# Softmax divided on a^T behind the attention, position tables fetched during the fold, full-height Fourier tails

## Chip, cores and metric

The kernel runs on one core of a Trainium2 chip. The metric is device time in microseconds for one execution of the whole program, which is one encoder layer on two request batches. All of it is computed in fp32 precision: each operand of a large matmul is split into a rounded high part and a remainder, and three matmuls replace one (high times high, high times low, low times high).

## The reference, cut to what matters

```python
def encoder_layer(x, ...):                    # x_prompt: 256 + 16 meta tokens, x_sample: 1024 + 16, d_model 1024
    h = rms_norm(x, norm_mix_g)
    z = h @ w_in                              # q 512 | k 128 | v 128 | f 512 | gate logits 1024 + 1024
    ...
    g_attn = jax.nn.sigmoid(z[..., o3:o4]); g_four = jax.nn.sigmoid(z[..., o4:])
    q = axial_rope(head_rms_norm(q, q_norm_g), row, col); k = ...     # 8 query heads, 2 kv heads, head_dim 64
    a = bidirectional_gqa(q, k, v) @ w_attn_o
    fo = fourier_mix(f) @ w_four_o
    x = x + (g_attn * a + g_four * fo) @ w_out
    h2 = rms_norm(x, norm_ffn_g); u = h2 @ w_ffn_in                   # d_ff 2816
    return x + (jax.nn.silu(u[..., :D_FF]) * u[..., D_FF:]) @ w_ffn_out

def attention_block(qb, k, v):
    s = jnp.einsum('bqhgd,bshd->bhgqs', qb, k) * scale
    p = jax.nn.softmax(s, axis=-1)
    return jnp.einsum('bhgqs,bshd->bqhgd', p, v)

def fourier_mix(f):                           # 4 groups of 128 channels
    return jnp.real(jnp.fft.fftn(f.reshape(b, l, 4, 128), axes=(1, 3), norm='ortho')).reshape(b, l, 512)
```

## The kernel before

The work runs in stages. Tokens stand in three chunks: 0 and 1 are the 1024 sample tokens, 2 the 256 prompt tokens; tiles 0 to 7 are the sample's 128-row tiles, 8 and 9 the prompt's. Most tiles in on-chip memory are slots of one pool, and a new user of a slot waits for the last user of the old one. The order of instructions on an engine is the order in which the program's generators write them, except inside manual blocks, where it is written out; `weave` and `Filler` mix a main generator with a side generator by cost shares. SyncE (SP) issues most DMAs, one queue in order; GpSimd (POOL) issues the position tables.

- Up to 65 us the tokens are normalized and transposed (hT). `folds` adds and subtracts mirrored positions (tiles ep, od, then eo as high and low parts). `fourier_in` multiplies these with the channel matrix wc into six banks u, and then casts the banks into `ue` and `uo` (the even and odd parts, high on ScalarE, low on VectorE). The fifth bank has 41 rows.
- `fourier` multiplies the position tables with ue and uo: `tabp` for the prompt (outputs fpe, fpo, rows 128 and 41), `tabc` and `tabs` for the sample (fse and so on, rows 4 x 128 and 9). Their DMAs are issued behind fourier_in, `tabs` at the second of the kinds. `gate_gen` makes the gate logits g, one unit of weights (wg, cast to wgh, remainder wgl) at a time: chunk 0 is woven into the Fourier, q and kv passes (shares 0.6, 0.35, 0.7), chunks 1 and 2 fill the attention by `FILL`, in ns per yield.
- Attention handles the prompt tiles first, then the sample. For a tile, a kv group g and four heads it makes the scores S (one buffer), their negated maximum (L954), the exponential p with its row sum (L961), and, one head later, `scale`: a reciprocal (L965) and p times it (L966). `Second` and `product` then transpose p (pt, pT) and multiply with v (pv, ao), and store a^T to a_d.
- `load_af` reads a_d back and splits it (afh, afl) for the merge; chunks 0 and 2 are started at the end of the attention, chunk 1 inside the merge. `merge` runs over eight column blocks i: `fourier(i + 1)` (fo), then m for chunks 0, 2, 1; `need` prepares the weights wm two blocks ahead, behind the first m. `w_out` follows; its first weight unit is split by GpSimd (woh, wol).
- ffn_in and ffn_out fill the time from 905 us to the end.

Of the kernel before, what the change touches and what calls it, by code (L numbers as in the profile page):

```python
# [9 lines left out]
F32 = mybir.dt.float32  # L10
F32R = mybir.dt.float32r
# [125 lines left out]
def f32(ap):  # L137
    return ap.bitcast(F32)
# [44 lines left out]
class Kernel:  # L183
    def __init__(self, tc, nc, a, o, pools):
        self.tc, self.nc, self.a, self.o = tc, nc, a, o
        self.const, self.small, self.dram, big = pools
        self.later = None
        self.sl = Slots(big, N_SLOTS, N_TRIPLES)
        c = self.const
        self.ident = c.tile([P, P], F32, name="ident")  # L190
        nc.scalar.dma_start(self.ident[:], a["ident"])
        self.gcol = c.tile([P, KD], F32, name="gcol")
        self.mhalf = c.tile([P, NQH], F32, name="mhalf")
        nc.vector.memset(self.mhalf[:], -0.5)
        self.gates = [
            [self.dram.tile([P, n], F32, name=f"gate{u}_{i}") for i, n in enumerate(CH_N)]
            for u in range(16)
        ]
        self.x_d = [self.dram.tile([P, D], F32, name=f"x_d{t}") for t in range(10)]
        self.act_d = [[self.dram.tile([P, 640], F32, name=f"act_d{j}_{k}") for k in range(NH)] for j in range(7)]  # L200
        self.q_d = [self.dram.tile([P, D], F32, name=f"q_d{t}") for t in range(10)]
        self.a_d = [self.dram.tile([512, n], F32, name=f"a_d{i}") for i, n in enumerate(CH_N)]


        self.f_d = self.dram.tile([516, NL], F32, name="f_d")
# [291 lines left out]
            yield  # L497
        sl.put(*hs, ep, od)

    def fourier_in(self, ps):  # L500

        nc, sl = self.nc, self.sl
        cols = [(j * P, P) for j in range(4)] + [(512, 41), (553, P)]
# [1 line left out]
        for k in range(KD):  # L505
# [16 lines left out]
                sl.put(*x)  # L522
            if k + 2 < KD:
                next(self.fold)
            if k % 2:
                sl.put(*self.wc[k // 2])
        next(self.fold, None)
        ue = [sl.get("ue", F32R) for _ in range(3)]
        uo = [sl.get("uo", F32R) for _ in range(3)]
        for x in uo:  # L530
            nc.gpsimd.memset(f32(x.v(4, 256))[:, :, 252:256], 0.0)
        for j, (_, m) in enumerate(cols):
            ev = banks[j][:m, :260].rearrange("p (g c) -> p g c", g=4)
            b = j % 2 * 520
            u = ue[j // 2]
            for base, w, src in ((0, 64, ev[:, :, :64]), (256, 1, ev[:, :, 64:65])):
                hv = u.v(4, w, b + base)[:m]
                lv = u.v(4, w, b + 260 + base)[:m]
                nc.scalar.copy(hv, src)
                nc.vector.tensor_tensor(lv, src, f32(hv), op=ALU.subtract)  # L540
            b = j % 2 * 512
            u = uo[j // 2]
            src = banks[j][:m, 260:512]
            nc.scalar.copy(u[:m, b : b + 252], src)
            nc.vector.tensor_tensor(u[:m, b + 256 : b + 508], src, f32(u[:m, b : b + 252]), op=ALU.subtract)
        self.U = ue, uo
        yield 6000

    FILL = {"s": 455, "p": 350, "end": 480, "drain": 900}

    def gate_gen(self, chunks, lo_engine):

# [56 lines left out]
    def fourier(self, ps):  # L611
        nc, a, sl = self.nc, self.a, self.sl
        tp = [sl.get(f"tabp{j}", F32R) for j in range(2)]
        for j, m in enumerate((P, 41)):
            nc.gpsimd.dma_start(tp[j][:m, : 4 * NLP], a["pos_p"][j, :m])
        yield from self.fourier_in(ps)
        us = self.U

        def u_e(uu, j, m, p, part):
# [24 lines left out]
            nc.sync.dma_start(self.f_d[row : row + m, lo : lo + n], st[:m, :n])  # L644


        ms = [P, 41]
        for kind, p in kinds:
            rows = 4 if kind == "4" else P
            pf = ps.tile([P, 512], F32, tag="mm", name=f"fp{kind}{p}")  # L650
# [12 lines left out]
        sl.put(*tp)  # L663


        ms = [P, P, P, P, 9]
        tabs = {}

        def tab(name):
            tabs[name] = [sl.get("tab" + name, F32R) for _ in range(5)]  # L670
            for j, m in enumerate(ms):
                nc.gpsimd.dma_start(tabs[name][j][:m, :1040], a["pos_" + name][j, :m])

        tab("c")
        for i, (kind, p) in enumerate(kinds):
            if i == 1:
                tab("s")
# [173 lines left out]
    def attention(self, ps, tiles, tag_s, tag_v):  # L851
# [64 lines left out]
            )  # L916
            sl.put(aos)

        queue, n, scale, S = deque(), 0, None, None

        def turns(k):

# [9 lines left out]
        for i, (t, g) in enumerate(units):  # L932
# [5 lines left out]
                seq, L, cuts = "p", LP, (0, LP)  # L938
            per = SLOT // L
            ps4, slots = [], []  # L940
            for h in range(4):
                hq = q[t][:, (4 * g + h) * P : (4 * g + h + 1) * P]

# [9 lines left out]
                nb, total, rc = sm[:, 0:1], sm[:, 1:2], sm[:, 2:3]  # L953
                nc.vector.tensor_reduce(nb, S[:, base : base + L], axis=AX.X, op=ALU.max, negate=True)  # L954
                turns(0)
                if scale:
                    scale()
                if h % per == 0:
                    slots.append(sl.get("p"))
                p = slots[-1][:, (h % per) * L : (h % per + 1) * L]  # L960
                self.last_exp = nc.scalar.activation(p, S[:, base : base + L], AF.Exp, bias=nb, accum_out=total)  # L961
                yield "end" if i + 1 == len(units) else seq, 0, False

                def scale(p=p, rc=rc, total=total):
                    nc.vector.reciprocal(rc, total)  # L965
                    nc.vector.tensor_scalar(p, p, rc, None, op0=ALU.mult)  # L966

                ps4.append(p)
                turns(1)
# [9 lines left out]
        scale()  # L979
        while queue:  # L980
            for half in range(2):
                turns(half)
# [52 lines left out]
    def load_af(self, c):  # L1035

        nc, sl = self.nc, self.sl
        n = CH_N[c]
        per = 1024 // n
        out = self.af[c] = []  # L1040
        raws = {}

        def load(i):
            if i < 4 // per:
                raws[i] = sl.get("af")
                src = self.a_d[c][i * per * P : (i + 1) * per * P, :].rearrange("(k p) n -> p k n", p=P)
                nc.sync.dma_start(raws[i].v(per, n), src)

        load(0)
        load(1)  # L1050
        yield 1
        for i in range(4 // per):
            raw = raws.pop(i)
            out.append(self.split(raw, 1024, "af", nc.vector, "t"))
            sl.put(raw)
            yield 1

    def merge(self, then):
# [106 lines left out]
        load_gates(2)  # L1165
        for i in range(8):
            yield from fourier(i + 1)
            if i == 0:
                run_all(self.last_af)
            if i == 5:  # L1170
# [6 lines left out]
            for c in (0, 2, 1):  # L1177
# [11 lines left out]
                    self.three(pm[:, :n], [(wk, mv)], k == 0, k == 3)  # L1189
                    yield 3 * n / 2.4  # L1190
                if c == 0:
                    need(i + 2)
                    load(i + 3)
                v = gt[:, n : 2 * n]
                nc.vector.tensor_tensor(v, pm[:, :n], v, op=ALU.mult)
# [22 lines left out]
    def w_out(self, tiles, ps, then=None, apart=False):  # L1218
# [476 lines left out]
    def build(self):  # L1695
# [3 lines left out]
        with self.psum("pb", {"mm": 4, "tr": 2, "g": 2}) as ps:  # L1699
# [209 lines left out]
```

## Time and profile before

| what | us |
|---|---|
| median of 3 runs (1738.76, 1736.38, 1736.07) | 1736.38 |
| profiled execution, its own time | 1737.35 |
| span of that execution | 1735.6 |
| TensorE busy / VectorE / ScalarE / GpSimd | 1672.8 / 1137.2 / 723.0 / 299.7 |
| mean granted TensorE clock | 0.988 of full speed |

A row of the timeline reads: start, duration, engine, line, operation, output and inputs by the program's names, shape, and in brackets the idle time of that engine before it with what released it. A row of the waits reads: who waited, for whom, us in total, times, longest. A window's PEclk is the mean clock that the throttle granted to TensorE.

### The profile page before, as it was taken

To read this page: it belongs to the slowest core of one execution; us is meant where nothing else is said; L and a number is where in the kernel's file an instruction comes from. 1 tells how busy PE (TensorE), PEld (TensorE's weight loads), DVE (VectorE), ACT (ScalarE), POOL (GpSimd) and SP (SyncE) were. 2 spreads that over 40 slices of the span, in tenths; PEclk is the share of its full clock that TensorE was granted. 3 is DMA by queue.
4 is the path that set the end of the run, shared out by engine and by line. 5 is a ranking of instruction groups with operands and counts; after the bars stand their busy time and mean duration, and the time that the engine had idled before them with its cause. 6 is when DMAs were issued, how large, how long until landed. Compare 5 with 4: busy or idle time off the path is not lost.

```text
span 1735.6 us, 25870 instructions
## 1 busy us (share of the span) xinstructions
PE 1672.8 (96%) x9789; PEld 1489.0 (86%) x9789; DVE 1137.2 (66%) x2086; ACT 723.0 (42%) x1462; POOL 299.7 (17%) x347
## 2 busy tenths in 40 slices
PE   7998999999999999989989999999999999999998
PEld 7897888877787878878879999999999998888886
DVE  5562454357888886652379766667666768665685
ACT  6432333355666666451355222222232224444444
POOL 3440233311002111663353000000000000000002
PEclk9997999999999999999999999999999999999999
DMA  6124232221111217534442222322232237553534
GB/s 245 39 106 134 100 122 91 80 79 57 44 59 45 67 56 231 169 108 143 150 166 77 86 69 95 102 90 83 94 102 90 70 119 256 196 182 101 159 98 152
DMA packets 90541, 195.77 MB, mean 113 GB/s; under 512 B 9773, under 2 KB 41161, under 8 KB 90416
## 3 DMA queue, kind: packets, MB, share of 16 engines
q1 hardware_dynamic: 80592, 176.88, 31.0%
q10 hardware_dynamic: 8400, 12.53, 2.0%
q0 software_dynamic: 1424, 4.70, 0.8%
q8 instruction: 77, 1.26, 0.3%
q14 instruction: 48, 0.39, 0.1%
HBM read 138.65 MB, written 55.42 MB: 112 GB/s over the span
## 4 chain that ended last, share of the span: by engine, by line
PE 60%; DVE 6%; issue 3%; ACT 3%; POOL 2%; DMA 1%; POOLq 0%; ACTq 0%; SPq 0%; DVEq 0%
PE i L231 10%; PE i L229 10%; PE i L230 10%; PE o L231 5%; PE o L230 5%; PE o L229 4%; PE S L949 3%; PE pt L883 2%; PE wo L230 1%; PE pv L903 1%; PE wo L231 1%; PE wo L229 1%; PE pv L904 1%; PE g L229 1%; POOL gt L1196 1%
## 5 line engine op out<-in xcount | busy, mean ns | idle before, releaser
L1402 ACT CAST w<-wi 128x512 fp32r<-128x512 f32 x168 | 104.0, 621 | 270.5 <-PE i L231 216.5
L229 PE MATMUL i<-A,w 128*128 128x384 f32 x616 | 208.6, 339 | 3.0 <-ACT w L1402 2.7
L231 PE MATMUL i<-A,w 128*128 128x384 f32 x616 | 208.4, 339 | 2.4 <-POOL w L1404 2.3
L230 PE MATMUL i<-A,w 128*128 128x384 f32 x616 | 208.2, 338 | 0.0
L229 PE MATMUL i<-Ah,w 128*128 128x256 f32 x616 | 173.6, 282 | 0.9 <-DVE sc L1458 0.7
L231 PE MATMUL i<-Ah,w 128*128 128x256 f32 x616 | 173.7, 282 | 0.0
L230 PE MATMUL i<-Al,w 128*128 128x256 f32 x616 | 173.3, 281 | 0.0
L238 POOL TENSOR_SCALAR fin0r<-fin0ss 128x1 f32<-128x1 f32 x1 | 0.8, 785 | 757.5 <-ACT X L246 757.5
L885 ACT CAST pT<-pt 128x512 fp32r<-128x512 f32 x156 | 90.5, 580 | 89.6 <-PE pt L883 87.6
L886 DVE TENSOR_TENSOR pT<-pt,pT 128x512 fp32r<-128x512 f32 x156 | 106.9, 686 | 26.9 <-ACT pT L885 25.1
L1404 DVE TENSOR_TENSOR w<-wi,w 128x512 fp32r<-128x512 f32 x154 | 105.3, 685 | 29.0 <-ACT w L1402 28.6
L229 PEld LDWEIGHTS i<-A,w 128*128 128x128 f32 x616 | 116.7, 190 | 3.6 <-ACT w L1402 2.9
L231 PEld LDWEIGHTS i<-A,w 128*128 128x128 f32 x616 | 116.5, 189 | 3.1 <-POOL w L1404 3.1
L229 PEld LDWEIGHTS i<-Ah,w 128*128 128x128 f32 x616 | 116.3, 189 | 1.6 <-DVE sc L1458 0.9
L230 PEld LDWEIGHTS i<-Al,w 128*128 128x128 f32 x616 | 116.5, 189 | 0.0
L230 PEld LDWEIGHTS i<-A,w 128*128 128x128 f32 x616 | 116.5, 189 | 0.0
L231 PEld LDWEIGHTS i<-Ah,w 128*128 128x128 f32 x616 | 116.4, 189 | 0.0
L954 DVE TENSOR_REDUCE sm<-S 128x1 f32<-128x1040 f32 (+1 forms) x80 | 86.4, 1080 | 41.0 <-PE S L949 35.1
L961 ACT ACTIVATE p<-S,sm 128x1040 f32<-128x1040 f32 (+1 forms) x80 | 80.1, 1001 | 35.3 <-DVE sm L954 30.9
L883 PE MATMUL pt<-ident,p 128*128 128x128 f32 (+1 forms) x624 | 93.7, 273 | 0.0
L231 PE MATMUL o<-wfo,act 128*128 128x512 f32 (+1 forms) x212 | 82.2, 388 | 1.6 <-DVE act L1536 1.6
L230 PE MATMUL o<-wfo,act 128*128 128x512 f32 (+1 forms) x212 | 82.1, 387 | 0.2 <-DVE wfo L1540 0.2
(734 smaller groups left out, 4470.5 us busy)
## 6 DMA issues: line engine op xcount, KB each, us to landing
wi<-w_fi SPq DMA_DIRECT2D x48, 512.0 KB
act_d<-sc SPq DMA_DIRECT2D x77, 192.0 KB
wg<-w_g SPq DMA_DIRECT2D x24, 512.0 KB
act<-act_d SPq DMA_DIRECT2D x37, 320.0 KB
wfo<-w_fo SPq DMA_DIRECT2D x21, 512.0 KB
X<-act_d SPq DMA_DIRECT2D x31, 320.0 KB
act_d<-sc SPq DMA_DIRECT2D x77, 128.0 KB
gt<-gate SPq DMA_DIRECT2D x32, 256.0 KB
```

Source lines behind the costliest of these rows:

```text
L229: mm(out, sh, mh, start=first and i == 0, stop=False)
L230: mm(out, sh, ml, start=False, stop=False)
L231: mm(out, slo, mh, start=False, stop=last and i == n - 1)
L883: nc.tensor.transpose(pt[:rows, h * P : (h + 1) * P], me.ps4[h][:, col : col + rows], self.ident[:])
L885: nc.scalar.copy(pT[:rows, :512], pt[:rows, :])
L886: nc.vector.tensor_tensor(pT[:rows, 512:1024], pt[:rows, :], f32(pT[:rows, :512]), op=ALU.subtract)
L903: nc.tensor.matmul(me.pv[:], vst, pT[:rows, :512], start=j == 0, stop=False)
L949: nc.tensor.matmul(S[:, base + lo : base + hi], hq, self.kT[seq][g][v][:, lo:hi], start=v == 0, stop=v == 1)
L954: nc.vector.tensor_reduce(nb, S[:, base : base + L], axis=AX.X, op=ALU.max, negate=True)
L961: self.last_exp = nc.scalar.activation(p, S[:, base : base + L], AF.Exp, bias=nb, accum_out=total)
L1402: nc.scalar.copy(w[:, :512], src)
L1404: eng.tensor_tensor(w[:, 512:1024], src, f32(w[:, :512]), op=ALU.subtract)
```

## The change

Seven things change.

1. `scale` is gone. The four row sums of a unit go into one tile `total`; once per unit one reciprocal of 128x4 is taken, and two DMAs of four-byte elements store it transposed to a new array `rc_d`. `load_af` reads it back, broadcast over 64 partitions, and VectorE multiplies the a^T tile by it before the split. The second load of a chunk is issued a step later.
2. The position tables of the sample are fetched piece by piece during the fold (`tab`), and the gate generator is started once ahead of everything (`next(gates)`), so that the first gate weights are loaded and cast during the fold.
3. The tails of 41 and 9 rows become 128 rows; GpSimd clears the tiles first.
4. fourier_in ends with a cost of 8000 instead of 6000, so that more gate matmuls are written ahead of the first fpe.
5. The woven shares fall from 0.35 to 0.28 and from 0.7 to 0.62; FILL is 420 instead of 455 for the sample and 500 instead of 350 for the prompt.
6. In the merge, `need(i + 2)` stands ahead of the m matmuls for i of 1 and more.
7. The first split of w_out moves to VectorE, and `next(then)` from the second chunk of the last block to the first.

```diff
+        self.rc_d = [self.dram.tile([2, 4 * n], F32, name=f"rc_d{i}") for i, n in enumerate(CH_N)]
...
     def fourier_in(self, ps, tab):
...
+            elif k + 2 == KD:
+                next(self.fold, None)
+            for _ in range((0, 0, 2, 0, 2, 0, 4, 2)[k]):
+                tab()
             if k % 2:
                 sl.put(*self.wc[k // 2])
-        next(self.fold, None)
...
-        for x in uo:
+        for x in uo[:2]:
             nc.gpsimd.memset(f32(x.v(4, 256))[:, :, 252:256], 0.0)
+        nc.gpsimd.memset(f32(ue[2][:, :520]), 0.0)
+        nc.gpsimd.memset(f32(uo[2][:, :1024]), 0.0)
...
-        yield 6000
+        yield 8000
...
-    FILL = {"s": 455, "p": 350, "end": 480, "drain": 900}
+    FILL = {"s": 420, "p": 500, "end": 480, "drain": 900}
...
+        def tab():
+            name = "c" if len(tabs["c"]) < 5 else "s"
+            j = len(tabs[name])
+            t = sl.get("tab" + name, F32R, "s")
+            tabs[name].append(t)
+            if j == 4:
+                nc.gpsimd.memset(f32(t[:, :1040]), 0.0)
+            m = P if j < 4 else 9
+            nc.gpsimd.dma_start(t[:m, :1040], a["pos_" + name][j, :m])
...
-        ms = [P, 41]
+        ms = [P, P]
...
-        ms = [P, P, P, P, 9]
+        ms = [P] * 5
...
+            total = self.small.tile([P, 4], F32, tag="total", name=f"total{t}{g}", bufs=3)
             for h in range(4):
...
                 turns(0)
-                if scale:
-                    scale()
+                if divide and h == 1:
+                    divide()
+                    divide = None
...
-                def scale(p=p, rc=rc, total=total):
-                    nc.vector.reciprocal(rc, total)
-                    nc.vector.tensor_scalar(p, p, rc, None, op0=ALU.mult)
...
+            def divide(t=t, g=g, total=total):
+                c, off = t // 4, t % 4 * P
+                nc.vector.reciprocal(total[:], total[:])
+                for x in range(2):
+                    dst = self.rc_d[c][x].rearrange("(k n) -> n k", k=4)[off : off + P, 2 * g : 2 * g + 2]
+                    nc.sync.dma_start(dst, total[:, x::2])
...
         def load(i):
             if i < 4 // per:
-                raws[i] = sl.get("af")
+                r, d = raws[i] = sl.get("af"), sl.get("rc")
...
+                for x in range(2):
+                    src = self.rc_d[c][x, i * 1024 : (i + 1) * 1024]
+                    nc.sync.dma_start(d[x * HD : (x + 1) * HD, :1024], src.partition_broadcast(HD))
 
         load(0)
-        load(1)
         yield 1
         for i in range(4 // per):
-            raw = raws.pop(i)
-            out.append(self.split(raw, 1024, "af", nc.vector, "t"))
+            load(i + 1)
+            r, d = raws.pop(i)
+            nc.vector.tensor_tensor(r[:, :1024], r[:, :1024], d[:, :1024], op=ALU.mult)
+            out.append(self.split(r, 1024, "af", nc.vector, "t"))
...
             yield from fourier(i + 1)
+            if i:
+                need(i + 2)
...
                 if c == 0:
-                    need(i + 2)
+                    if i == 0:
+                        need(2)
                     load(i + 3)
...
-                if c == 2 and i == 7:
+                if c == 0 and i == 7:
                     next(then)
...
-        units[0] = self.split(raw, 1024, "wo", nc.gpsimd, "s")
+        units[0] = self.split(raw, 1024, "wo", nc.vector, "s")
...
+            next(gates)
             weave(ahead(self.fourier(ps), QSTART, q_pass), gates, 0.6)
-            weave(ahead(q_pass, KVSTART, kv_pass), gates, 0.35)
-            weave(kv_pass, gates, 0.7)
+            weave(ahead(q_pass, KVSTART, kv_pass), gates, 0.28)
+            weave(kv_pass, gates, 0.62)
```

ScalarE at the end of fourier_in, before the change: the last casts of the fold (eo), two pairs of gate weight casts (wgh), then the first u banks.

```order
L494 CAST eo_1490<-ep_999 128x681
L494 CAST eo_1496<-od_1000 128x681
L571 CAST wgh_1619<-wg_1617 128x512 x2
L571 CAST wgh_1634<-wg_1625 128x512 x2
L539 CAST ue_1572<-u_1164 128x256
L539 CAST ue_1572<-u_1164 128x4
L544 CAST uo_1575<-u_1164 128x252
L539 CAST ue_1572<-u_1165 128x256
```

The same place after the change:

```order
L496 CAST eo_1511<-ep_1002 128x681
L496 CAST eo_1517<-od_1003 128x681
L546 CAST ue_1607<-u_1177 128x256
L546 CAST ue_1607<-u_1177 128x4
L551 CAST uo_1610<-u_1177 128x252
L546 CAST ue_1607<-u_1178 128x256
L546 CAST ue_1607<-u_1178 128x4
```

The casts of gate weights no longer stand between the fold and the evacuation of u.

TensorE at the end of the kv pass, before: the last kv matmul, the transposes ktr of the last two key tiles, then the first scores S of the attention and a gate group.

```order
L231 MATMUL kv_3457<-wkvh_2482,hT1l_687 128x256
L790 MATMUL ktr_3516<-ident,ks_3441 128x128 x4
L790 MATMUL ktr_3525<-ident,ks_3509 128x128 x4
L949 MATMUL S_3554<-kTp_2756,qT_3550 128x272 x2
L229 MATMUL g_1_3561<-hT1h_684,wgh_3536 128x512
L230 MATMUL g_1_3561<-hT1h_685,wgh_3536 128x512
L231 MATMUL g_1_3561<-hT1h_684,wgl_3537 128x512
```

After the change the first of the two ktr groups is followed by gate matmuls of chunk 0:

```order
L233 MATMUL kv_3432<-wkvh_2476,hT1l_690 128x256
L800 MATMUL ktr_3490<-ident,ks_3416 128x128 x4
L231 MATMUL g_0_3325<-hT0h_259,wgh_3175 128x512
L232 MATMUL g_0_3325<-hT0l_260,wgh_3175 128x512
L233 MATMUL g_0_3325<-hT0h_259,wgl_3176 128x512
```

and they go on, 24 in all, up to the last ktr group:

```order
L231 MATMUL g_0_3505<-hT0h_259,wgh_3370 128x512
L232 MATMUL g_0_3505<-hT0l_260,wgh_3370 128x512
L233 MATMUL g_0_3505<-hT0h_259,wgl_3371 128x512
L800 MATMUL ktr_3527<-ident,ks_3483 128x128 x4
L231 MATMUL g_0_3505<-hT0h_259,wgh_3370 128x512
```

The two ktr groups stand 24 gate matmuls apart, where nothing stood between them.

VectorE from the last weights of the first merge block on, before (L214 is the split of an a^T tile, L1138 and L1139 sum and difference of the Fourier output):

```order
L1096 TENSOR_TENSOR pT_6243<-wmf_6751,pT_6243 128x512
L1096 TENSOR_TENSOR pT_6243<-wma_6754,pT_6243 128x512
L214 TENSOR_TENSOR afl_6984<-af_6765,afh_6983 128x1024
L214 TENSOR_TENSOR afl_6992<-af_6767,afh_6991 128x1024
L214 TENSOR_TENSOR afl_6998<-af_6995,afh_6997 128x1024
L1138 TENSOR_TENSOR fst_7033<-fst_7033,fo_7026 128x328
L1139 TENSOR_TENSOR fst_7033<-fst_7033,fo_7026 128x328
L1138 TENSOR_TENSOR fst_7054<-fst_7054,fo_7047 128x192
```

The same place after the change (L216 is the split, L1073 the multiply by the reciprocals; af_6699 and af_6914 are chunk 0, af_6934 is chunk 2):

```order
L1116 TENSOR_TENSOR pT_6185<-wma_6688,pT_6185 128x512
L1073 TENSOR_TENSOR af_6699<-af_6699,rc_6700 128x1024
L1158 TENSOR_TENSOR fst_6976<-fst_6976,fo_6969 128x328
L1159 TENSOR_TENSOR fst_6976<-fst_6976,fo_6969 128x328
L216 TENSOR_TENSOR afl_6921<-af_6699,afh_6920 128x1024
L1073 TENSOR_TENSOR af_6914<-af_6914,rc_6915 128x1024
L1158 TENSOR_TENSOR fst_6997<-fst_6997,fo_6990 128x192
L1159 TENSOR_TENSOR fst_6997<-fst_6997,fo_6990 128x192
L1158 TENSOR_TENSOR fst_6997<-fst_6997,fo_6990 128x136
L1159 TENSOR_TENSOR fst_6997<-fst_6997,fo_6990 128x136
L216 TENSOR_TENSOR afl_6931<-af_6914,afh_6930 128x1024
L1073 TENSOR_TENSOR af_6934<-af_6934,rc_6935 128x1024
```

The three splits that stood together now stand apart, each behind a multiply, with Fourier work between.

More of the change, by code (lines that the diff above doesn't have):

```diff
@@ L498, in folds, with fourier_in @@
         sl.put(*hs, ep, od)
-    def fourier_in(self, ps):
+    def fourier_in(self, ps, tab):
         nc, sl = self.nc, self.sl
@@ L613, in fourier @@
         tp = [sl.get(f"tabp{j}", F32R) for j in range(2)]
-        for j, m in enumerate((P, 41)):
-            nc.gpsimd.dma_start(tp[j][:m, : 4 * NLP], a["pos_p"][j, :m])
-        yield from self.fourier_in(ps)
+        for j in range(2):
+            nc.gpsimd.dma_start(tp[j][:, : 4 * NLP], a["pos_p"][j])
+        tabs = {"c": [], "s": []}
+        def tab():
[7 more added lines that the diff above has]
+            nc.gpsimd.dma_start(t[:m, :1040], a["pos_" + name][j, :m])
+        yield from self.fourier_in(ps, tab)
         us = self.U
@@ L663, in fourier @@
         sl.put(*tp)
-        ms = [P, P, P, P, 9]
[L667 to L674, printed above, removed]
+        ms = [P] * 5
         for i, (kind, p) in enumerate(kinds):
-            if i == 1:
-                tab("s")
             rows = 4 if kind == "4" else P
@@ L917, in product @@
             sl.put(aos)
-        queue, n, scale, S = deque(), 0, None, None
+        queue, n, divide, S = deque(), 0, None, None
         def turns(k):
@@ L952, in attention @@
                 sm = self.small.tile([P, 4], F32, tag="sm", name="sm", bufs=4)
-                nb, total, rc = sm[:, 0:1], sm[:, 1:2], sm[:, 2:3]
+                nb = sm[:, 0:1]
                 nc.vector.tensor_reduce(nb, S[:, base : base + L], axis=AX.X, op=ALU.max, negate=True)
                 turns(0)
-                if scale:
-                    scale()
+                if divide and h == 1:
+                    divide()
+                    divide = None
                 if h % per == 0:
@@ L960, in attention @@
                 p = slots[-1][:, (h % per) * L : (h % per + 1) * L]
-                self.last_exp = nc.scalar.activation(p, S[:, base : base + L], AF.Exp, bias=nb, accum_out=total)
+                self.last_exp = nc.scalar.activation(p, S[:, base : base + L], AF.Exp, bias=nb, accum_out=total[:, h : h + 1])
                 yield "end" if i + 1 == len(units) else seq, 0, False
-                def scale(p=p, rc=rc, total=total):
-                    nc.vector.reciprocal(rc, total)
-                    nc.vector.tensor_scalar(p, p, rc, None, op0=ALU.mult)
                 ps4.append(p)
@@ L978, in attention @@
             queue.append((Second(t, g, ps4, slots), n + 1))
-        scale()
+            def divide(t=t, g=g, total=total):
[4 more added lines that the diff above has]
+                    nc.sync.dma_start(dst, total[:, x::2])
+        divide()
         while queue:
@@ L1044, in load @@
             if i < 4 // per:
-                raws[i] = sl.get("af")
+                r, d = raws[i] = sl.get("af"), sl.get("rc")
                 src = self.a_d[c][i * per * P : (i + 1) * per * P, :].rearrange("(k p) n -> p k n", p=P)
-                nc.sync.dma_start(raws[i].v(per, n), src)
+                nc.sync.dma_start(r.v(per, n), src)
+                for x in range(2):
+                    src = self.rc_d[c][x, i * 1024 : (i + 1) * 1024]
+                    nc.sync.dma_start(d[x * HD : (x + 1) * HD, :1024], src.partition_broadcast(HD))
         load(0)
-        load(1)
         yield 1
         for i in range(4 // per):
-            raw = raws.pop(i)
-            out.append(self.split(raw, 1024, "af", nc.vector, "t"))
-            sl.put(raw)
+            load(i + 1)
+            r, d = raws.pop(i)
+            nc.vector.tensor_tensor(r[:, :1024], r[:, :1024], d[:, :1024], op=ALU.mult)
+            out.append(self.split(r, 1024, "af", nc.vector, "t"))
+            sl.put(r, d)
             yield 1
```

## Prediction

> **What bounds the kernel now.** I read the page first: the engine totals.
>
> ```profile
> PE 1672.8 (96%) x9789; PEld 1489.0 (86%) x9789; DVE 1137.2 (66%) x2086; ACT 723.0 (42%) x1462; POOL 299.7 (17%) x347
> ```
>
> TensorE is busy 1672.8 of 1735.6 us, and the change neither adds nor removes a matmul. It can only win the other 62.8 us, the stretches at a low clock, and slow matmul forms. So I next asked for the waits of TensorE in five stretches (120 to 280, 280 to 420, 420 to 660 and 660 to 800 us; us in total, times, longest):
>
> ```profile
> PE fpe L229 <- ACT ue L539: 4.5, 1, 4.5
> ...
> PE S L949 <- ACT p L961: 4.8, 6, 1.5
> PE ktr L790 <- DVE ks L779: 3.0, 2, 2.7
> ...
> PE pv L903 <- DVE ao L911: 4.1, 6, 0.9
> ...
> PE fo L229 <- ACT wm L1095: 2.5, 4, 0.8
> ...
> PE fo L231 <- DVE wm L1096: 0.6, 4, 0.2
> ```
>
> and then for windows over the stages that the change touches (length, PE, PEld, DVE, ACT, POOL busy, granted clock, DMA share, GB/s):
>
> ```profile
> 140.00:160.00 20.00, 20.00 (x85) 16.65 (x83) 1.61 (x5) 2.10 (x4) 0.00 (x0) 0.60 0.20 63
> 340.00:404.00 64.00, 58.29 (x321) 46.86 (x320) 35.83 (x81) 31.64 (x76) 10.32 (x8) 0.97 0.24 77
> 404.00:672.00 268.00, 260.20 (x1558) 215.03 (x1558) 225.39 (x336) 172.11 (x311) 36.56 (x32) 1.00 0.21 65
> 672.00:720.00 48.00, 45.76 (x266) 40.12 (x265) 32.45 (x61) 29.31 (x55) 22.78 (x31) 1.00 0.68 213
> ```
>
> The attention is idle 5.7 us in its prompt part (340 to 404) and 7.8 in its sample part (404 to 672), and 140 to 160 runs full at clock 0.60. Those are the prizes; 672 to 720, where the change adds VectorE work, is already tight.
>
> **A, start of the Fourier stage.** The timeline there:
>
> ```profile
> 123.85 0.28 PE L519 MATMUL u<-wch,eo 128*128 128x252 f32 x1
> ...
> 126.41 1.14 ACT L571 CAST wgh<-wg 128x512 fp32r<-128x512 f32 x2 [1.65 <-DMA wg<-w_g]
> 127.46 0.36 ACT L539 CAST ue<-u 128x256 fp32r<-128x256 f32 x1
> ...
> 135.88 0.36 ACT L539 CAST ue<-u 128x256 fp32r<-128x256 f32 x1
> ...
> 136.29 0.48 PE L229 MATMUL fpe<-hT0l,ue 128*128 128x136 f32 x1 [4.46 <-ACT ue L539]
> ...
> 155.33 0.42 PE L229 MATMUL fse<-tabc,ue 128*128 128x260 f32 x1
> 155.55 0.41 PE L230 MATMUL fse<-tabc,ue 128*128 128x260 f32 x1
> ...
> 156.40 0.28 PE L230 MATMUL fse<-tabc,ue 128*128 128x260 f32 x1
> 156.52 0.28 PE L231 MATMUL fse<-tabc,ue 128*128 128x260 f32 x1
> 156.73 0.38 PE L229 MATMUL fse<-tabc,ue 9*128 9x260 f32 x1
> ...
> 157.28 0.50 PE L229 MATMUL g<-hT0h,wgh 128*128 128x512 f32 x1
> ```
>
> The first u bank is complete at 124.1 (123.85 + 0.28), but ScalarE stands behind casts of gate weights that land late, so the evacuation of six banks runs 127.46 to 136.24 (8.8 us) and the first fpe waits 4.46. After the change the first gate's weights are loaded and cast during the fold, and nothing stands ahead of the evacuation: 124.1 + 8.8 = 132.9. 24 gate matmuls stand ahead of fpe instead of 18: 127.5 + 24 x 0.23 = 133.0 (a 512-column matmul follows another in 0.23, quoted under E, and in 0.43 at half clock, under B). The wait goes: -4.4. With it goes the half clock, which lasts from 136.3 to 155.7 (260-column matmuls follow each other in 0.22 there and in 0.12 from 155.9 on, a factor 1.8): 19.4 x (1 - 1/1.8) = -8.6. The Trainium skill ("TensorE: Matmul & The Clock Gate", Part 1) has the clock halve after an idle window of about 3.4 us and return after 3.4 us of busy time; the 4.46 us agree with the first, the 19.4 us at half clock under a full TensorE with the second not at all, and by it this term would be -1.5 instead of -8.6.
>
> Tails: a 9-row group costs 0.76 (156.52 to 157.28) where four full-height matmuls at 0.12 cost 0.48, so 0.28 x 10 groups = 2.8; five 41-row groups in the prompt part, bounded by 0 and the same 0.28, 0.7: together -3.5. Cover: four large memsets on GpSimd and the table DMAs, now between the fold's additions. They wait for u matmuls to free their slots, and the fold's last additions queue behind them; the fold is ahead of u (ScalarE idles before 126.41), so I price this at 0, bounds 0 and +3 (two such additions).
> A = -4.4 - 8.6 - 3.5 = -16.5.
>
> **B, end of the kv pass.** 24 gate matmuls (5.5 us) now stand between the last two ktr groups.
>
> ```profile
> 339.43 0.82 PE L790 MATMUL ktr<-ident,ks 128*128 128x128 f32 x4 [2.70 <-DVE ks L779]
> ...
> 343.05 0.63 PE L229 MATMUL g<-hT1h,wgh 128*128 128x512 f32 x1
> 343.48 0.43 PE L230 MATMUL g<-hT1h,wgh 128*128 128x512 f32 x1
> ```
>
> They cover the wait of 3.0, and the half clock of 340.0 to 343.5 goes: 3.5 x (1 - 0.23/0.43) = 1.6, with the ktr 2.0. Against that, q and kv tiles get fewer gates between them (0.28 and 0.62 for 0.35 and 0.7): bounds 0 to +3, I take +1. B = -4.
>
> **C and D, attention.** One head of the sample:
>
> ```profile
> 501.07 1.12 PE L949 MATMUL S<-kT,qT 128*128 128x264 f32 x6
> ...
> 502.22 1.24 DVE L954 TENSOR_REDUCE sm<-S 128x1 f32<-128x1040 f32 x1 [0.45 <-PE S L949]
> ...
> 503.98 0.15 DVE L965 RECIPROCAL sm<-sm 128x1 f32<-128x1 f32 x1
> 504.16 0.76 DVE L966 TENSOR_SCALAR p<-p,sm 128x1040 f32<-128x1040 f32 x1
> 504.85 1.22 PE L949 MATMUL S<-kT,qT 128*128 128x264 f32 x6 [0.16 <-ACT p L961]
> ```
>
> The change takes 0.91 us of VectorE from each of 64 sample heads (58 of its 225 us there) and gives back 20 short reciprocals. VectorE is not the bound, so this is worth only what TensorE waits for it: pv behind ao (4.1), and the S waits. FILL moves gates: 16 prompt heads x 2 yields x 0.15 = 4.8 us in, 64 x 2 x 0.035 = 4.5 us out of the sample heads. TensorE's work per sample head falls from 260.2/64 = 4.07 to 4.00; the chain S, reduce, exponential, next S takes 504.85 less 501.07 = 3.78 and holds S back only below that. I take 4 of 5.7 in the prompt part and 4.5 of 7.8 in the sample part (bounds 0 and all). C + D = -8.5.
>
> The stores of reciprocals, 40 on SP's queue, carry 256 four-byte elements each.
>
> ```profile
> q1 hardware_dynamic: 80592, 176.88, 31.0%
> ```
>
> That queue's packets took 1735.6 x 16 x 0.31 / 80592 = 0.107 us each, so 10240 more take 68 us of all 16 DMA engines, in a stretch with a share of 0.21. Nobody on the path waits for them before the a^T multiply; behind them in the queue stand gate weights, loaded a unit ahead. Priced 0.
>
> **E, from attention to merge.** Now the five a^T tiles are multiplied on VectorE (no row; the nearest is the split, the same 128x1024 with two inputs), each after 2 more loads, and splits that were done in one run come behind casts:
>
> ```profile
> 683.12 3.03 ACT L213 CAST afh<-af 128x1024 fp32r<-128x1024 f32 x3
> ...
> 684.20 3.50 DVE L214 TENSOR_TENSOR afl<-af,afh 128x1024 fp32r<-128x1024 f32 x3 [0.18 <-ACT afh L213]
> ...
> 695.16 0.40 PE L229 MATMUL m<-wm,pT 128*128 128x512 f32 x1
> 695.39 0.39 PE L230 MATMUL m<-pT 128*128 128x512 f32 x1
> ```
>
> By the old clock VectorE is free at 684.0. Five multiplies and five splits at 1.17 to 1.22, three casts of 1.0 that nothing covers and 4.5 us of fst work (0.29 to 0.50 each) end at 704.4; before, all was split by 695.3. TensorE waits 0.7 for the third a^T tile's lo part, reaches chunk 1 (695.16 before) at 695.9 and waits until 699.6 (3.7), for its lo part (1.1), its second half (1.1, 1.0) and the next wm (1.3): +8.9. The ten rc loads add 2.6 MB, 12 us at the 213 GB/s of that window; a little of it will show: E = +10, bounds 0 (VectorE's freed time draws it forward) and +20.
>
> **F, merge loop.** wm for step i + 2 is prepared ahead of the m matmuls from i = 1: the waits for wm, 2.5 + 0.6, go: -3. **G, w_out.**
>
> ```profile
> 778.71 0.50 PE L229 MATMUL wo<-woh,afl 128*128 128x512 f32 x1 [1.68 <-ACT woh L213]
> 781.49 0.79 PE L230 MATMUL wo<-wol,afl 128*128 128x512 f32 x1 [2.28 <-POOL wol L214]
> ...
> 787.20 0.44 PE L231 MATMUL wo<-woh,afl 128*128 128x512 f32 x1
> ...
> 779.10 2.34 POOL L214 TENSOR_TENSOR wol<-wo,woh 128x1024 fp32r<-128x1024 f32 x1
> ...
> 782.62 1.23 DVE L214 TENSOR_TENSOR wol<-wo,woh 128x1024 fp32r<-128x1024 f32 x1 [4.08 <-ACT woh L213]
> ```
>
> The split moves from GpSimd (2.34 there) to VectorE (1.23) and starts about 1.3 us earlier: the two waits, 4.0, become 1.9, and the half clock of 781.5 to 787.3 should go (5.8 x 0.46 = 2.7). G = -4.8.
>
> **Sum.** -16.5 - 4 - 8.5 + 10 - 3 - 4.8 = -26.8. The profiled execution took 1737.35 us (span 1735.6), 1 us over the median of 1736.4; from the median, 1709.6: **1710**.
>
> **Rivals.** (1) The evacuation still starts after the last u (127.7): fpe at 136.5, a gap of 3.4 behind the 24 gates, and the clock falls. For: it was a gap of 4.46 that did it. Against: the cast at 127.46 began before the last u matmul had ended. Loses 3.4 + 8.6: 1722. (2) The merge start costs more: the clock halves in E's gap of 3.7, as at wo (5.8 us at half, 2.7), and rc loads that stand behind gt loads are late by up to 12: 1713 to 1724, about 1718. The same page of the Trainium skill ("Why this matters for your kernels") warns of gaps over about 3 us between matmul bursts, so by it the 2.7 fall due here. The clock of 1.00 from 404 to 672, with pv waits up to 0.9, shows only that short ones do no harm. (3) E is hidden, since VectorE has 58 us less to do ahead of it: E = 0 to 2, 1701. (4) The relief is not what it says: S has one buffer, its 3.78 chain binds, C + D = 0: 1718. (5) The other side: the four-byte stores hold SP's queue. If a pair goes through few engines (512 x 0.107 = 55 us over one, 3.4 over 16), gate weights come late and TensorE loses its filler. It decides from 27/20 = 1.35 us per pair; at 2 us, 1736 + 40 - 27 = 1750. For: SP issues in order. Against: DMA share 0.21. The Trainium skill ("DMA: Bandwidth & Descriptors", Specifications) puts writes under 512 bytes at a read-modify-write each; no row here shows its price.
>
> **Chances.** Forecast 0.44, (1) 0.13, (2) 0.18, (3) 0.11, (4) 0.09, (5) 0.05. The range takes in all but (5) and the edges of (1) to (3): 1699 to 1723. 0.2% (3.5 us) is about what can be told from no change. (5) gives slower 0.05; (1) and (2) together with less gain in the attention come near no change, 0.04; the rest is faster, 0.91.
>
> **What would show it.** Right: no wait over 1 us at the first fpe and clock 1.00 in the 20 us behind it; ktr without its wait; no pv wait on ao; new waits of m on afh and afl behind the attention, 7 to 10 us in sum; the first wo waits 2 us, at full clock. Wrong: any half clock left in the Fourier stage, waits of gates for weights in the attention, m waiting for a DMA. A merge start over 20 us would break the range.

## The result and the profile after

The changed kernel takes 1834.35 us (median of 4 runs, 1824.47 to 1836.16) against 1736.22 before: a ratio of 1.0555 (95% interval 1.0513 to 1.0597). It is 98 us slower where 26 us of gain were forecast. The profiled execution spans 1832.3 us. Its page, totals, clock and DMA parts:

```profile
PE 1692.9 (92%) x9789; PEld 1503.1 (82%) x9789; DVE 1090.4 (60%) x1953; ACT 723.6 (39%) x1462; POOL 302.4 (17%) x348
...
PEclk9999999999988899789999999999999999999999
...
DMA packets 102302, 198.63 MB, mean 108 GB/s; under 512 B 20806, under 2 KB 52194, under 8 KB 102176
...
q1 hardware_dynamic: 92272, 179.54, 36.2%
```

TensorE stands idle 139 us instead of 63, and the low clock has moved from the Fourier stage (the fourth digit before the change) into the attention and the start of the merge. q1 carries 11680 packets and 2.7 MB more than before, and its share rose from 31.0% to 36.2% of a longer span.

Where the time went shows in the first S, the first fo and the first wo row of TensorE in each timeline. They cut the span into four stages. The table has them for the profiled execution of the main runs (all us; the runs are told below).

| run | up to attention | attention | merge | from w_out | median |
|---|---|---|---|---|---|
| before | 340.0 | 340.8 | 97.9 | 956.9 | 1736.2 |
| after | 323.6 | 447.7 | 107.8 | 953.1 | 1834.4 |
| e1, no stores | 325.0 | 344.2 | 108.5 | 953.0 | 1731.9 |
| e2, stores in rows | 323.8 | 347.0 | 108.6 | 952.0 | 1734.4 |
| e3, division on p | 323.2 | 344.8 | 96.6 | 953.8 | 1720.9 |
| e4, before plus stores | 339.7 | 419.8 | 97.6 | 956.6 | 1814.8 |
| e9, e3 with old FILL | 323.6 | 339.6 | 97.9 | 952.4 | 1714.5 |
| e10, e1 without multiplies | 323.7 | 343.9 | 97.9 | 951.5 | 1718.7 |
| e15, e10 with old FILL | 323.6 | 339.8 | 97.9 | 952.1 | 1715.2 |

After against before: -16.4, +106.9, +9.9, -3.8. Everything outside the attention went roughly as forecast; the attention lost 107 us. TensorE's waits there, in the windows 280 to 420, 420 to 560, 560 to 700 and 700 to 860:

```profile
PE S L960 <- ACT p L973: 10.4, 7, 5.6
PE S L960 <- DMA qT<-q_d: 2.4, 1, 2.4
...
PE pt L893 <- DVE pT L896: 13.2, 5, 6.3
PE S L960 <- ACT p L973: 12.8, 2, 11.6
...
PE pt L893 <- DVE pT L896: 15.9, 3, 7.3
PE S L960 <- ACT p L973: 6.4, 2, 5.7
...
PE pt L893 <- DVE pT L896: 21.9, 2, 11.6
```

Before, no wait of TensorE in the attention was longer than 1.5 us. Now there are waits of 6 to 12 on VectorE, which has less to do than before (1090.4 us for 1137.2), and on ScalarE, which has as much (723.6 for 723.0). What these wait for stands in the waits of all engines from 340 to 740 ("remote" is a releaser that the profile can't place):

```profile
ACT pT L895 <- remote: 34.8, 6, 8.2
ACT pT L895 <- DMA a_d<-ao: 20.4, 2, 13.1
ACT pT L895 <- DMA rc_d<-total: 13.5, 1, 13.5
```

ScalarE's cast of p^T takes a slot of the pool, and the last user of that slot can be the store of a^T, which now ends late. Before the change no wait of this kind stands in the attention. One such stall in the timeline:

```profile
502.36 0.59 SPq L924 DMA_DIRECT2D a_d<-ao  x1
...
503.05 1.08 SPq L993 DMA_DIRECT2D rc_d<-total  x2
...
510.18 0.28 PE L233 MATMUL g<-hT2h,wgl 128*128 128x256 f32 x1
520.30 0.58 ACT L895 CAST pT<-pt 128x512 fp32r<-128x512 f32 x1 [13.10 <-DMA a_d<-ao]
...
522.06 2.10 PE L960 MATMUL S<-kT,hT0l 128*128 128x264 f32 x6 [11.60 <-ACT p L973]
```

and in windows of 2 us (the last three columns are granted clock, DMA share, GB/s):

```profile
506.00:508.00 2.00, 2.00 (x12) 1.69 (x11) 0.71 (x2) 1.21 (x3) 0.00 (x0) 1.00 0.21 36
508.00:510.00 2.00, 2.00 (x16) 1.78 (x15) 1.24 (x1) 0.00 (x0) 0.00 (x0) 1.00 0.00 0
...
514.00:516.00 2.00, 0.00 (x0) 0.00 (x0) 0.00 (x0) 0.00 (x0) 0.00 (x0) 0.50 0.00 0
```

A unit's a^T store and the pair of reciprocal stores are issued at 502.4 and 503.1. The packets are through by 508; then the DMA engines show no packet at all, and still the release comes only at 520.3. In those 12 us TensorE runs dry, and its clock halves.

### The profile page after: what moved, and what is told of

Its sections match the earlier page's. It is cut to its first block, busy times and chain, and to the rows that moved or that the text cites. A ratio compares the mean times of both kernels' runs of the same rounds, so it can differ in the third digit from the quotient of the medians.

```text
span 1832.3 us, 25969 instructions
## 1 busy us (share of the span) xinstructions
PE 1692.9 (92%) x9789; PEld 1503.1 (82%) x9789; DVE 1090.4 (60%) x1953; ACT 723.6 (39%) x1462; POOL 302.4 (17%) x348
## 3 DMA queue, kind: packets, MB, share of 16 engines
q1 hardware_dynamic: 92272, 179.54, 36.2%
## 4 chain that ended last, share of the span: by engine, by line
PE 53%; DVE 7%; DMA 6%; ACT 3%; issue 3%; POOL 2%; another core or an unknown queue 2%; SPq 0%; ACTq 0%; POOLq 0%; DVEq 0%
PE i L233 9%; PE i L231 9%; PE i L232 9%; PE o L233 5%; PE o L232 5%; PE o L231 5%; PE S L960 3%; DMA rc_d<-total 2%; PE pt L893 2%; DMA a_d<-ao 1%; PE wo L232 1%; DVE sm L965 1%; PE wo L233 1%; PE wo L231 1%
## 5 line engine op out<-in xcount | busy, mean ns | idle before, releaser
L1425 ACT CAST w<-wi 128x512 fp32r<-128x512 f32 x168 | 104.0, 621 | 272.4 <-PE i L233 219.2
L896 DVE TENSOR_TENSOR pT<-pt,pT 128x512 fp32r<-128x512 f32 (+1 forms) x138 | 94.1, 686 | 134.3 <-ACT pT L895 128.6
L893 PE MATMUL pt<-ident,p 128*128 128x128 f32 (+1 forms) x624 | 102.3, 290 | 51.1 <-DVE pT L896 51.0
L895 ACT CAST pT<-pt 128x512 fp32r<-128x512 f32 (+1 forms) x138 | 79.2, 581 | 173.9 <-PE pt L893 92.6
L893 PEld LDWEIGHTS pt<-ident,p 128*128 128x128 f32 (+1 forms) x624 | 77.2, 143 | 66.0 <-DVE pT L896 56.2
L233 PE MATMUL o<-wfo,act 128*128 128x512 f32 (+1 forms) x212 | 82.1, 388 | 2.0 <-DVE act L1559 2.0
```

The costliest lines, as they stand in the source:

```text
L233: mm(out, slo, mh, start=False, stop=last and i == n - 1)
L893: nc.tensor.transpose(pt[:rows, h * P : (h + 1) * P], me.ps4[h][:, col : col + rows], self.ident[:])
L895: nc.scalar.copy(pT[:rows, :512], pt[:rows, :])
L896: nc.vector.tensor_tensor(pT[:rows, 512:1024], pt[:rows, :], f32(pT[:rows, :512]), op=ALU.subtract)
L1425: nc.scalar.copy(w[:, :512], src)
```

## The experiments

**e1: no stores.** The changed kernel without the two DMAs of `divide`; `rc_d` holds ones, so the result isn't normalized.

```diff
                 nc.vector.reciprocal(total[:], total[:])
-                for x in range(2):
-                    dst = self.rc_d[c][x].rearrange("(k n) -> n k", k=4)[off : off + P, 2 * g : 2 * g + 2]
-                    nc.sync.dma_start(dst, total[:, x::2])
```

> The changed kernel without the 40 stores of four-byte elements; the array of reciprocals is filled once with ones in rows at the start, so the result isn't normalized. All else stays: reciprocals, broadcast loads, multiplies, order. Theory S (the stores take the 107 us that the attention lost): attention about as forecast, 1705 to 1715 us in all. Rival F (the attention lost them by FILL, the gate shares or the new order): above 1800. Rival Q (half and half): 1760 to 1790.

1731.93 us, ratio to before 0.9977 (0.9965 to 0.9989). The attention falls from 447.7 to 344.2 us: the 40 stores cost 102 us in all. But 1732 isn't 1710. Without the stores the change gains only 4 us, so a second part of the forecast is wrong too.

**e2: the same bytes in rows.** TensorE transposes the four sums, VectorE takes the reciprocal from there, and each unit stores four rows of 512 bytes.

```diff
-                nc.vector.reciprocal(total[:], total[:])
-                for x in range(2):
-                    dst = self.rc_d[c][x].rearrange("(k n) -> n k", k=4)[off : off + P, 2 * g : 2 * g + 2]
-                    nc.sync.dma_start(dst, total[:, x::2])
+                pt = ps.tile([P, 512], F32, tag="tr", name=f"tt{t}{g}")
+                nc.tensor.transpose(pt[:4, :P], total[:], self.ident[:])
+                rt = sl.get("rt", F32, "s")
+                nc.vector.reciprocal(rt[:4, :P], pt[:4, :P])
+                for j in range(2):
+                    dst = self.rc_d[c][:].rearrange("x (k n) -> k x n", k=4)[2 * g + j, :, off : off + P]
+                    nc.sync.dma_start(dst, rt[2 * j : 2 * j + 2, :P])
```

> The changed kernel, with the row sums of a unit turned on TensorE (128x4 to 4x128), the reciprocal taken from there, and the same 2 KB stored as four rows of 512 bytes: 4 descriptors instead of 512 per unit. Theory S with the size of the elements as the cause: 1706 to 1716, since the transposes cost 20 x 0.1 us. Rival: any store of the reciprocals at this place in SP's queue hurts, whatever its form: above 1780.

1734.41 us, ratio 0.9994 (0.9981 to 1.0007): 100 us better than the change at the same place in SP's queue, and no better than the kernel before. A store there is no harm; its form is.

**e3: division back on p.** `scale` as before, `load_af` as before, no `rc_d`; all other parts of the change stay.

> The changed kernel with the division back on p (one head later, as before), no reciprocals stored or loaded, a^T not multiplied; all other parts of the change stay. From the trace after: start of attention -16, w_out -3, merge start without the multiplies about -3, attention about as before or up to 5 better or worse by FILL: 1710 to 1722. If the other parts are worth nothing: 1736.

1720.94 us, ratio 0.9918 (0.9889 to 0.9946). The other parts are worth 14 us, and the division on a^T, even without its stores (e1), loses 11 of them again.

**e4: only the stores.** The kernel before, with the exponentials' sums in one tile per unit, and that tile stored in four-byte elements to an array that nobody reads.

> The kernel before with nothing added but the 40 stores of four-byte row sums to an array that nobody reads. Theory S: the attention loses about 107 us here too, 1825 to 1855. Rival (the stores hurt only together with the lighter VectorE or the broadcast loads): 1737 to 1760.

1814.78 us, ratio 1.0438 (1.0402 to 1.0474). The attention goes from 340.8 to 419.8. The stores alone do it, 10 us short of the expected range: 79 us here, where VectorE still has the division, and 102 in the changed kernel.

**e5, e6, e11, e14, e12: the same stores, farther apart.** All five are e1 with the 40 stores back, 256 four-byte elements each, into an unread array. Only the distance between elements differs (`w` = 16, 128, 4, 2, 1 words).

```diff
+        self.rx_d = [self.dram.tile([2, 4 * n, w], F32, name=f"rx_d{i}") for i, n in enumerate(CH_N)]
...
                 nc.vector.reciprocal(total[:], total[:])
+                for x in range(2):
+                    dst = self.rx_d[c][x, :, 0:1].rearrange("(k n) o -> n (k o)", k=4)[off : off + P, 2 * g : 2 * g + 2]
+                    nc.sync.dma_start(dst, total[:, x::2])
```

> As the run without stores (e1), but with 40 stores of 256 four-byte elements again, now into an array that nobody reads, each element 64 bytes from the next. Theory L (neighbouring four-byte writes into the same line of memory wait for each other): the attention stays near e1's 344 us, 1730 to 1745 in all. Rival N (each small write costs, wherever it goes): attention about 440, 1815 to 1840.

> The same with the elements 512 bytes apart. Theory L with a line of 512 bytes instead of 64: near 1732 here and slow in e5. Rival N: 1815 to 1840 here too.

> As the run with elements 64 bytes apart (e5), but 16 bytes apart, four to 64 bytes. If writes into one line of 64 bytes wait for each other: a part of the loss, about a quarter, 1750 to 1765. If only direct neighbours or a smaller line matter: 1731. All of it, above 1815, if the line is larger than 64 bytes, which e5 speaks against.

> As e5 and e12, with the elements 8 bytes apart, eight to 64 bytes. 16 bytes apart cost nothing, 4 bytes apart cost about 85 us. If the cost goes by writes per 64 bytes: still 1732 or a part of it. If it needs two writes in the same 16 bytes: about half the loss or more, 1770 to 1815.

> The control to e5 and e11: the same stores into the same unread array with the elements 4 bytes apart, as in the changed kernel. Expected 1815 to 1840; if it stays near 1732, the loss in the changed kernel comes from the array being read later, not from the spacing.

| bytes apart | 512 | 64 | 16 | 8 | 4 |
|---|---|---|---|---|---|
| run | e6 | e5 | e11 | e14 | e12 |
| us | 1731.4 | 1730.9 | 1734.6 | 1740.3 | 1817.0 |
| against e1 (1731.9) | -0.5 | -1.0 | +2.7 | +8.4 | +85.1 |
| attention | 345.7 | 344.1 | 348.2 | 352.0 | 427.9 |

This is the plainest result of the study: 10240 four-byte writes cost nothing when they lie 64 bytes apart, and 85 us when they touch (the 2.7 us at 16 bytes are at the edge of the scatter). e12 also shows that nobody has to read the array. Where the other 17 us of the changed kernel's 102 come from, no run shows. The queue row of e5, e14 and e12 (packets, MB, share of 16 engines' span) has the same packets and bytes in all three:

```profile
q1 hardware_dynamic: 92272, 179.54, 31.7%
```

```profile
q1 hardware_dynamic: 92272, 179.54, 33.2%
```

```profile
q1 hardware_dynamic: 92272, 179.54, 36.7%
```

With e1's 31.5% of 1730.7 us as the base, the packets of the queue took longer in all by 0.005, 0.046 and 0.18 us for each of the 10880 added ones (e5, e14, e12). This is not the duration of one write, since other packets of the queue can have grown too (e8 below). The 8 us of e14 are not lost within the attention's loop but at its end: the reduction of the last sample head comes 318.8 us after that of the first prompt head, for 318.2 in e1, and behind it VectorE waits 7.5 us (2.0 in e1) for merge weights that stand behind the stores. In e12 the loop itself grows, from 318.2 to 374.5 us. The expectation of a quarter of the loss at 16 bytes was wrong: the time lost rises far faster than the number of writes per 64 bytes, which only doubles from one column to the next between 16, 8 and 4 bytes.

**e7: 128 elements of 16 bytes per unit**, contiguous, the same 2 KB in one store.

> As e1, with one store per unit of 128 elements of 16 bytes, contiguous in memory (the same 2 KB, a quarter of the elements). If the cost goes by the number of elements, a quarter of the loss: attention about 344 + 25, 1752 to 1762. If it goes by bytes or runs: as with the four-byte stores, 1815 to 1840. If only sizes of four bytes are slow: 1732.

1729.6 us, ratio 0.9964 (0.9951 to 0.9977): no loss. Neither bytes nor runs are slow. These elements touch too, and they start 16 bytes apart as those of e11 do; what goes with the loss is four-byte elements that start 4 bytes apart, and a little those that start 8 bytes apart.

**e8: the stores on GpSimd's queue.** `nc.sync` becomes `nc.gpsimd` for them in the changed kernel.

> The changed kernel with the 40 four-byte stores issued by GpSimd on its own queue instead of SP's. If the loss comes from SP's queue (what stands behind the stores waits its turn): 1735 to 1760. If it comes from the memory or the DMA engines, which both queues share: 1800 to 1840.

1814.37 us, ratio 1.0459 (1.0428 to 1.0489). Moving them off SP's queue saves 20 us of the 102. What stalls is mostly shared by both queues: ScalarE's casts still wait 20.3 us for a^T stores on SP's queue (20.4 in the changed kernel). The queue row, and the DMA rows with the median time from issue to landing, which the profile has for GpSimd's queue alone:

```profile
q1 hardware_dynamic: 81392, 179.50, 36.2%
...
tabs<-pos_s POOLq DMA_DIRECT2D x4, 520.0 KB, 5.2
...
rc_d<-total POOLq DMA_DIRECT2D x40, 1.0 KB, 12.6
```

A store of 1 KB lands 12.6 us after its issue, a table load of 520 KB after 5.2. And q1, which has exactly the packets of e1 here and none of the stores, still shows 36.2% of 1811.0 us for 31.5% of 1730.7: its own packets took 1770 us of engine time longer, nearly as much as the 1930 of e12 with the stores among them. So in e8 the added packet time lies on packets that have nothing to do with the stores; in e12 the same may hold for most of it.

**e10: nothing divided.** e1 also without the multiplies and the broadcast loads of `load_af`.

```diff
-            nc.vector.tensor_tensor(r[:, :1024], r[:, :1024], d[:, :1024], op=ALU.mult)
...
-                for x in range(2):
-                    src = self.rc_d[c][x, i * 1024 : (i + 1) * 1024]
-                    nc.sync.dma_start(d[x * HD : (x + 1) * HD, :1024], src.partition_broadcast(HD))
```

> The run without stores (e1, 1731.9 us) also without the ten broadcast loads and the five multiplies, so nothing is divided anywhere. If the multiplies and their loads cost the merge's 12 us: from attention to w_out 96.5 as in e3 instead of 108.5, 1719 to 1722 in all. And since VectorE is then 60 us lighter than in e3 with all else equal, this run against e3 is the worth of the relief: 0 if pv and S wait for chains and not for VectorE's load, -8 by the forecast (1712).

1718.68 us, ratio 0.9907 (0.9891 to 0.9922). The merge stage falls from 108.53 to 97.87: the multiplies and their loads cost 10.7 us. Against e3 the attention is 0.9 us shorter, with 60 us less on VectorE.

**e9 and e15: FILL back at 455 and 350**, in e3 (division on p) and in e10 (no division).

```diff
-    FILL = {"s": 420, "p": 500, "end": 480, "drain": 900}
+    FILL = {"s": 455, "p": 350, "end": 480, "drain": 900}
```

> The version with the division back on p (e3, 1720.9 us), and FILL back at 455 and 350; fold, tails, woven shares, merge and w_out stay changed. If the new FILL is what makes e3's attention 344.8 us long against 340.8 before: 341 and 1717 in all. If those 4 us are the half clock and the q load at the attention's start: no change, 1719 to 1723.

> No division anywhere (e10) with FILL back at 455 and 350, against e9, which is the same with the division on p. VectorE is some 60 us lighter and nothing else differs. Forecast of the prediction (pv and S waits fall with VectorE's load): 8 us faster than e9, 1706. If these waits are chains through ScalarE and one buffer: within 2 us of e9's 1714.5.

1714.48 us (0.9888, 0.9867 to 0.9908) and 1715.17 us (0.9883, 0.9867 to 0.9900). The new FILL costs 5.2 us of attention (344.8 to 339.6). With the old one the relief of VectorE is still worth nothing: 339.8 without any division, 339.6 with it. Where the FILL's cost lies is seen in the windows of the prompt part and the sample part, cut at the reduction of the first and of the last sample head. First e9 (old FILL), then e3 (new):

```profile
323.58:365.65 42.07, 39.67 (x219) 32.42 (x220) 20.91 (x58) 20.18 (x54) 7.77 (x6) 0.96 0.29 90
365.65:638.02 272.37, 261.95 (x1556) 215.28 (x1555) 228.21 (x339) 174.97 (x315) 37.55 (x33) 1.00 0.17 52
```

```profile
323.19:369.61 46.42, 44.96 (x248) 37.30 (x249) 20.78 (x58) 21.05 (x56) 8.25 (x7) 0.96 0.30 98
369.61:642.48 272.87, 258.62 (x1526) 210.07 (x1525) 229.49 (x339) 174.21 (x313) 38.81 (x34) 1.00 0.17 50
```

The gate matmuls moved into the prompt part make it 4.3 us longer and fill only 0.9 us of its idle time. The sample part gives nothing back: TensorE has 3.3 us less to do there, and the part is 0.5 us longer. e9 is the best version found and beats both kernels: 21 us under before. It is the change without its first point and without the new FILL.

## Right and wrong, point by point

**The stores (priced 0): the step that failed.** The prediction worked out 68 us of DMA engine time and then set the price at zero, because nobody on the path reads `rc_d` before the merge. The runs put the price at 102 us (e1). Two links were wrong. The price of a packet was taken from a queue whose packets average 2.2 KB (176.88 MB in 80592), and an added packet of touching four-byte writes cost the queue 0.18 instead of 0.107 us, on itself or on others, with a landing 12.6 us after the issue (e8). And "nobody waits" looked only for readers. The waiting came through memory that is used again. One way is the slots whose last user was the a^T store beside these stores: 20.4 us of the waits of ScalarE's casts have that name, 13.5 have the reciprocal store's, and 34.8 none that the profile can place. By the program the sum tiles, which the stores read, are a second way; a wait of the exponential on them stands only in e4, 3.8 us in four times.

Rival (5) was the case that came true, with a chance of 0.05 and 1750 us. Its mechanism was only partly right: SP's order isn't what decides (e8), its price of 2 us per pair was 102 / 20 = 5.1, and the sign that it named, gates waiting for weights, isn't among TensorE's waits. The Trainium skill ("DMA: Bandwidth & Descriptors", Specifications) has transfers under 512 bytes done as a read-modify-write. In these runs that alone has no measurable price (e5, e6, e7); the price comes when four-byte writes touch.

**A, Fourier stage: nearly right.** The evacuation no longer stands behind weight casts, the wait at the first fpe is gone and the clock is full behind it:

```profile
121.64 0.38 PE L521 MATMUL u<-wch,eo 128*128 128x252 f32 x1 [0.71 <-DVE eo L497]
...
126.32 0.37 ACT L546 CAST ue<-u 128x256 fp32r<-128x256 f32 x1 [2.93 <-PE u L521]
...
129.67 0.39 PE L231 MATMUL g<-hT0h,hT0l 128*128 128x512 f32 x1
...
135.20 0.23 PE L231 MATMUL fpe<-tabp,ue 128*128 128x136 f32 x1
```

```profile
140.00:160.00 20.00, 19.23 (x134) 16.61 (x133) 3.48 (x9) 2.84 (x6) 0.00 (x0) 1.00 0.39 120
```

The u matmuls, however, end 2.1 us later (gates start at 129.67 instead of 127.53): the fold, with table DMAs and memsets between its additions, is now late for u. TensorE waits 1.9 us for eo, in three waits, where it waited for none. Which of the additions to the fold delays it, no run separates. That was the cover priced at 0 with a bound of +3. Rival (1) didn't happen.

**B, end of the kv pass: not gained.** The wait for ks fell from 2.70 to 0.49, but three gate matmuls later the first S waits 2.40 for the load of q, which is not ready so early, and the half clock is back (matmuls of 0.63):

```profile
319.71 0.81 PE L800 MATMUL ktr<-ident,ks 128*128 128x128 f32 x4 [0.49 <-DVE ks L789]
...
323.62 0.79 PE L960 MATMUL S<-kTp,qT 128*128 128x272 f32 x2 [2.40 <-DMA qT<-q_d]
...
325.07 0.63 PE L233 MATMUL g<-hT1h,wgl 128*128 128x512 f32 x1
```

A new wait took the place of the old one. A and B together gave -16.4 for a forecast of -20.5.

**C and D, attention: wrong, -8.5 forecast, 0 from the relief and +5 from FILL.** The prediction put pv's waits for ao down to VectorE's load. e3 and e10, with and without 60 us of it, have the same row between 420 and 660 (and with the old FILL, e9 and e15 both have 3.2 us in five times):

```profile
PE pv L912 <- DVE ao L920: 4.9, 8, 0.8
```

```profile
PE pv L917 <- DVE ao L925: 4.9, 8, 0.8
```

pv has one buffer, and the wait is the chain that empties it, a copy on ScalarE and an addition on VectorE, as in e10:

```profile
495.36 0.58 ACT L924 COPY ao<-pv 64x512 f32<-64x512 f32 x1
...
495.98 0.68 DVE L925 TENSOR_TENSOR ao<-pv,ao 64x512 f32<-64x512 f32 x1
...
496.72 0.50 PE L917 MATMUL pv<-hT0l,v 128*128 128x512 f32 x1 [0.40 <-DVE ao L925]
```

VectorE starts 0.04 us after ScalarE ends; there was no queue to shorten. The FILL's term failed at another step: the sum took TensorE's work as the bound of a sample head, 4.07 us and then 4.00, with a chain of 3.78 below it. That 3.78 was one head; the 64 sample heads of before, e9 and e3 follow each other at 4.3 us on the average (273.4, 272.4 and 272.9 us for 63 steps), and less work for TensorE didn't shorten them. This was rival (4) in its effect. The waits that the profile names are more pv's (4.9 us) than those of S (2.1 in e3, 1.8 in e10); which chain holds the heads at 4.3 us stays open.

**E, merge start: right, +10 for 10.7 (e1 against e10).** The places are those of the sum, and the clock fell in the gap as rival (2) had it. In e1:

```profile
689.50 0.79 PE L235 MATMUL m<-wm,pT 128*128 128x512 f32 x1 [3.46 <-ACT wm L219]
...
695.08 0.80 PE L235 MATMUL m<-wm,pT 128*128 128x512 f32 x1 [1.74 <-ACT wm L219]
```

```profile
692.68 1.23 DVE L1074 TENSOR_TENSOR af<-af,rc 128x1024 f32<-128x1024 f32 x1 [1.90 <-DMA rc<-rc_d]
```

```profile
690.00:700.00 10.00, 7.24 (x17) 4.97 (x17) 6.13 (x9) 3.54 (x6) 1.37 (x2) 0.50 0.67 204
```

The gap of 3.46 us was forecast as 3.7; the multiply took 1.22 to 1.76 for an estimate of 1.22, and one reciprocal load was late by 1.9. TensorE's waits for the splits come to 7.1 us where the sum had 8.9, and the half clock, priced in a rival only, filled the rest: that the total met the forecast is in part luck. (The terms of the sum also end at 703.7 and not at 704.4.) By the Trainium skill's warning of gaps over about 3 us ("TensorE: Matmul & The Clock Gate", Why this matters for your kernels) the half clock was due, but these traces don't bear out the 3 us as a bound: the clock also halved in a gap of 2.40 (first S, after) and in one of 2.28 that came behind one of 1.68 (first wo, before). In the gap of 3.46 it fell at 687.4, 1.4 us after TensorE had gone idle.

**F, merge loop: wrong, 0 instead of -3.** The waits for wm stayed (2.6 in e3 for 2.5 before, four times each). On VectorE nothing had moved, in e3 as before:

```profile
706.76 0.30 DVE L1148 TENSOR_TENSOR fst<-fst,fo 128x136 f32<-128x136 f32 x1
706.98 0.46 DVE L1100 TENSOR_TENSOR wmf<-wmf 128x256 f32<-128x256 f32 x1
```

```profile
719.58 0.30 DVE L1139 TENSOR_TENSOR fst<-fst,fo 128x136 f32<-128x136 f32 x1
719.79 0.48 DVE L1091 TENSOR_TENSOR wmf<-wmf 128x256 f32<-128x256 f32 x1
```

`need` stood directly behind the sums of fst already, because the m matmuls that it was moved past issue nothing on VectorE. The order of that engine would have told it.

**G, w_out: right**, about -4 for -4.8. The clock stays full there (1.00 from 880 to 890), and the two waits of 4.0 us are now these:

```profile
PE wo L232 <- DVE wol L216: 0.8, 1, 0.8
...
PE wo L231 <- ACT woh L215: 0.4, 1, 0.4
```

Put together for the change without its stores (e1 against before): -15.0 + 3.4 + 10.6 - 3.9 = -4.9. Of the forecast 26.8, 5.5 are missing in A and B, 12 in C and D, 3.6 in E and F, 0.9 in G.

What stays open: why touching four-byte writes are so slow. That writes to the same few bytes must follow each other in memory fits the steps from 16 to 8 to 4 bytes, but no run shows the memory itself. Nor was it tried which of the waits, slots or sum tiles, passes on more of the loss; the names in the traces speak for the slots.

## What to carry to other kernels

A transposed store of single words is not a small store: turn it on TensorE (e2) or leave a gap between the words (64 bytes in e5), and ask of a DMA not only who reads its target but who uses its source, and the sources of its neighbours in the queue, again. Before paying for lighter load on an engine, look whether the instruction that is waited for starts late because of a queue or at once when its input ends; only a queue gets shorter. When a step is moved in the program, compare the order on the engine that executes it.

## What was unexpected of the hardware

Four-byte writes to memory raised the packet time of their queue by 0.005 us for each added packet at 64 bytes apart, by 0.046 at 8 and by 0.18 side by side, for the same number of packets (e5, e14, e12). With the same stores on the other queue, the packets of the first still took nearly as much longer (e8), so there the time falls on packets other than the stores'. After a pair of stores of touching words the DMA engines showed no packet for 12 us (508 to 520) and the awaited release came only behind that, so the DMA share doesn't show the cost. Elements of 16 bytes side by side cost nothing (e7).
